# Two of four weight sums per quad formed by accumulating transfers

## The chip, the core and the metric

The kernel runs on one core of one Trainium2 chip. The metric is the time in microseconds of one execution on the device. Times of one kernel are compared as medians over runs, and where one profiled execution is read, its own time stands beside it.

## What is computed

One decoder block of a model with 1024 channels over 2048 positions, in float32:

```
proj = x @ W_in + b_in                      # 1024 -> 9216 columns
q, k, v, g_attn, u_lru, g_lru, gate_logits = split(proj)
A: rotary q, k; causal dilated window attention in 3 groups of 8 heads, merged by softmax weights,
   times silu(g_attn), @ w_attn_proj
B: width-4 causal conv of u_lru -> RG-LRU scan over positions, times silu(g_lru), @ w_lru_proj
merged = sigmoid(gA) * A + sigmoid(gB) * B
out = LayerNorm(2**0.25 * x + merged @ w_out + b_out)
```

Only the first line, `x @ W_in`, is touched by the change.

## The kernel before

The program has three stages. Stage A computes the input projection and starts what hangs on its columns (rotary parts, convolution and scan, gates). Stage B is the attention. Stage C merges and projects out. The change lies in stage A, about the first 1,550 us.

**The quad.** Stage A goes over the positions in two halves of 1024 columns and, in each half, over 36 pairs of 128-wide column tiles of `W_in`. One pair in one half is a quad: a 2 x 2 block product, with A the weights (A11 and A12 of the first tile, A21 and A22 of the second, each 128 x 512 and 256 KB) and B the positions. All but the first quad of each half are done by the Strassen-Winograd scheme, with 7 block products in place of 8. It needs four sums of weights: S1 = A21 + A22, S2 = S1 + A11, S3 = A21 + A11 and S4 = S2 + A12 (the second tile is taken with its sign turned, and `sgn` in `result` turns it back, so that all four are plain additions). `UNIT` names the weight block of each of the 7 products: A11, A12, S4, A22, S1, S2, S3. The order in a quad (`MID`) is A11, S2, S3, S1, A12, A22, S4.

Every block product is made of 12 matmuls of 128 x 512: each operand is split into a high half `h`, rounded to the matmul's format, and a low half `l`, the rest, and three of the four partial products are computed. `product` (line 577; its matmuls are line 592) issues them into one of four PSUM banks, and `evacuate` takes the bank out again on VectorE or ScalarE.

**The tick.** The whole of stage A is written out by a planner. One tick is one block product; `base[s]` is the tick at which quad s begins, and `at(t, fn)` puts an action into tick t. Each engine carries out its instructions in the order in which they are put there, so a tick fixes an order and not a time. Chains (`qk_chain`, `v_chain`, `lru` and others) take the results on; `spend` books their costs against a budget for each engine, which only decides in which tick a chain's next step is put. In the columns of u and g_lru (quads of kind "ug") the `lru` chain is started, in those of v the `v_chain`, whose four transposes `turn` stand on TensorE in the middle of a product.

**The weights of one quad.** With `t0 = base[s] - 4` in the first half and `base[s] - 3` in the second:

- `load_w` (line 237): SyncE loads A21 and A11 at t0 - 4, A22 and A12 at t0 - 3, each into one of 32 slots of 128 x 512 (`take`, `give`).
- `sums` (line 243), at t0 - 1: four additions, all on VectorE in the first half; in the second half S1 and S2 on VectorE, S3 and S4 on GpSimd (PoolE).
- `prep_w` (line 257), one for each of the seven blocks at t0 + j: ScalarE writes the high half (line 262). In the first half the low half follows, for even j on PoolE and for odd j on VectorE, and SyncE stores the low halves in `wl_scr` (line 279). In the second half SyncE loads them from there with `load_lo` (line 284).

All additions and subtractions are recorded by the helper `tt`, so they have line 232 in the profile, whatever they add; tiles tell them apart. `S<-wA,wA` is a sum of two loaded blocks (S3 and S1), `S<-S,wA` a sum with an earlier one (S2 and S4).

**Beside it.** At the start of each half the blocks of positions are split (`one_block`, line 221) and combined (`comb`: VectorE subtracts, ScalarE rounds, PoolE and VectorE write the low halves `xT`, line 221).

Of the kernel before, what the change touches and what calls it, by code (L numbers as in the profile page):

```python
# [8 lines left out]
F32 = mybir.dt.float32  # L9
F32R = mybir.dt.float32r  # L10
AF = mybir.ActivationFunctionType
ALU = mybir.AluOpType
# [3 lines left out]
P = 128  # L16
S = 2048
# [14 lines left out]
def hybrid_block_kernel(ctx: ExitStack, tc: tile.TileContext, a: dict, out: bass.AP):  # L32
    nc = tc.nc
    sp, act, dve, pool, pe = nc.sync, nc.scalar, nc.vector, nc.gpsimd, nc.tensor
# [111 lines left out]
    def take(name, dt=F32R):  # L146
        if not vacant:
            raise RuntimeError(f"no slot at {now['n']}: {[x[1].name if hasattr(x[1],'name') else x[1] for x in home.values()]} chains {len(chains)}")
        i = vacant.pop(0)
        t = sl_p.tile([P, CH], dt, tag=f"s{i}", name=name)  # L150
        home[id(t)] = (i, t)
        return t

    def give(*ts):
        for t in ts:
            vacant.append(home.pop(id(t))[0])
# [27 lines left out]
    def spend(**eng):  # L184
        for k, v in eng.items():
            left[k] = left.get(k, 0.0) - v
# [44 lines left out]
    def tt(eng, out, in0, in1, op):  # L231
        eng.tensor_tensor(out=out, in0=in0, in1=in1, op=op)  # L232


    U, LO, raw = {}, {}, {}

    def load_w(s, n):
        f = plan[s][1][int(n[1]) - 1][0]
        r = raw[s, n] = take(f"w{n}_{s}", F32)
        k = 4 * (int(n[2]) - 1)  # L240
        sp.dma_start(r.rearrange("p (k f) -> p k f", f=P), a["w_in"][f, :, k:k + 4, :])

    def sums(s):
        def add(n, x, y):
            t = raw[s, n] = take(f"{n}_{s}", F32)
            tt(pool if plan[s][0] and n in ("S3", "S4") else dve, t, raw[s, x], raw[s, y], ALU.add)
        add("S3", "A21", "A11")
        add("S1", "A21", "A22")
        give(raw.pop((s, "A21")))
        add("S2", "S1", "A11")  # L250
        add("S4", "S2", "A12")
        if plan[s][0]:
            spend(DVE=1.45, POOL=2.8)
        else:
            spend(DVE=2.9)

    def prep_w(s, j):

        n = units_of(s)[j]
        r = raw.pop((s, n))  # L260
        h = take(f"h{n}_{s}")
        act.activation(h, r, AF.Copy)  # L262
        spend(ACT=.66)
        if (s, j // 2) not in LO:
            LO[s, j // 2] = take_lo(f"l{j}_{s}")
        l = LO[s, j // 2][1][:, j % 2]
        if plan[s][2] is None or not plan[s][0]:
            eng = pool if j % 2 == 0 else dve
            tt(eng, l, r, flat(h), ALU.subtract)
            if eng is pool:  # L270
                spend(POOL=1.4)
            else:
                spend(DVE=.72)
        give(r)
        U[s, n] = (h, l)
        if plan[s][2] and not plan[s][0] and (j % 2 or j == 6):
            jj = j - j % 2
            t = LO[s, j // 2][1][:, 0:j - jj + 1]
            later(2, lambda: sp.dma_start(wl_scr[plan[s][3]][:, jj:j + 1], flat(t)))

    def load_lo(s, j):
        t = LO[s, j // 2] = take_lo(f"l{j}_{s}")
        n = 1 if j == 6 else 2
        sp.dma_start(flat(t[1][:, 0:n]), wl_scr[plan[s][3]][:, j:j + n])
# [240 lines left out]
    plan = []  # L525
# [116 lines left out]
    def at(t, fn):  # L642
        events.setdefault(t, []).append(fn)

    for s in range(1, NQ):
        t0 = base[s] - (3 if plan[s][0] else 4)
        for d, n in ((4, "A21"), (4, "A11"), (3, "A22"), (3, "A12")):
            at(t0 - d, lambda s=s, n=n: load_w(s, n))
        if plan[s][2] is None:
            for j in range(4):  # L650
                at(t0 + j, lambda s=s, j=j: prep_w(s, j))
            continue
        at(t0 - 1, lambda s=s: sums(s))
        for j in range(7):
            if plan[s][0] and j % 2 == 0:
                at(t0 + j - 1, lambda s=s, j=j: load_lo(s, j))
            at(t0 + j, lambda s=s, j=j: prep_w(s, j))
# [153 lines left out]
    sp2n = cst.tile([P, 8], F32, name="sp2n")  # L811
    left.update(PE=0.0, ACT=0.0, DVE=0.0, POOL=0.0)
    load_w(0, "A11")
    for kk in K4:
        load_raw("B11", 0, kk)
    load_w(0, "A12")
    for kk in K4:
        load_raw("B21", 0, kk)
# [49 lines left out]
    n = len(where)  # L868
# [145 lines left out]
    for m in range(NB + 4):  # L1014
        u, n = divmod(m, 16)
# [142 lines left out]
    for n in range(32):  # L1158
        c, f = divmod(n, 8)
# [23 lines left out]
    for j in range(3):  # L1183
        t = vx_p.tile([P, D], F32, name=f"vec{j}")
# [176 lines left out]
```

## Time and profile before

| | us |
|---|---|
| median of 3 runs | 2370.11 (2366.2 to 2374.58) |
| the profiled execution's own time | 2367.86 |
| span of its profile | 2366.1 |
| TensorE matmul busy | 2243.1 (95%) |
| VectorE busy | 1809.8 (76%) |
| ScalarE busy | 1086.5 (46%) |
| GpSimd busy | 953.3 (40%) |
| transfers, queue of SyncE | 64.9% of the 16 transfer engines' span |

The profile is one execution, read by the hardware profiler. PE is TensorE's matmul side and PEld its weight loads, DVE is VectorE, ACT ScalarE, POOL GpSimd, SP SyncE; a q behind an engine's name is its sequencer, which issues transfers. A wait is put down to the instruction or transfer that ended it. The time of a line is summed over the span, and an engine that stands idle costs nothing unless TensorE or the end waits for it.

### The profile page before, as it was taken

Reading aid. Unit: us, or ns where it says so; the run is one execution under the profiler, and the core shown is the slowest. Engines: PE = TensorE matmul, PEld = TensorE weight load, DVE = VectorE, ACT = ScalarE, POOL = GpSimd, SP = SyncE. Lnnn points to the kernel's source line nnn. Section 1 sums busy time; section 2 is a strip of 40 time slices with the busy share of each in tenths; the row PEclk is TensorE's granted clock in tenths of the full one; section 3 lists DMA queues with packets and bytes.
Section 4 is the critical chain, followed back from the end, with each engine's and each line's share of the span. In section 5 each row is a group of like instructions: output and inputs, shape, how many; then the busy total and the mean of one; then the engine's idle time right before and its main releaser. Section 6 shows DMA issues by size and latency. Waiting matters only on the chain. (4 is left out here: it accounts for less than half of the span.)

```text
span 2366.1 us, 34337 instructions
## 1 busy us (share of the span) xinstructions
PE 2243.1 (95%) x11008; PEld 1877.8 (79%) x11008; DVE 1809.8 (76%) x3221; ACT 1086.5 (46%) x1989; POOL 953.3 (40%) x655
## 2 busy tenths in 40 slices
PE   6999999999999999999999999999999999979998
PEld 4777777777777778888888788888999877758886
DVE  7988877888898778878879879745666558856677
ACT  4444244244344566647657657546666611121100
POOL 5443443443444623332323223378666326622220
PEclk8999999999999999999999999999999999999999
DMA  5665755766866967687687776797876579874431
GB/s 206 215 193 191 236 178 181 237 203 204 245 222 206 325 213 203 208 262 216 208 249 213 236 218 210 249 263 186 225 203 163 161 234 299 278 232 151 160 116 63
DMA packets 319237, 500.60 MB, mean 212 GB/s; under 512 B 95952, under 2 KB 136912, under 8 KB 314448
## 3 DMA queue, kind: packets, MB, share of 16 engines
q1 hardware_dynamic: 300384, 475.64, 64.9%
q10 hardware_dynamic: 18672, 22.75, 3.0%
q8 instruction: 88, 1.44, 0.3%
q14 instruction: 93, 0.76, 0.1%
HBM read 290.85 MB, written 182.26 MB: 200 GB/s over the span
## 5 line engine op out<-in xcount | busy, mean ns | idle before, releaser
L592 PE MATMUL q<-xT,hS 128*128 128x512 f32 x1680 | 525.5, 394 | 16.6 <-DVE y L232 10.3
L592 PE MATMUL q<-xT,l 128*128 128x512 f32 x1120 | 440.5, 393 | 0.5 <-DVE l L232 0.5
L592 PE MATMUL q<-xB,hA 128*128 128x512 f32 x1248 | 392.3, 396 | 22.3 <-ACT hA L262 14.8
L592 PEld LDWEIGHTS q<-xT,hS 128*128 128x128 f32 x1680 | 316.7, 190 | 88.3 <-issue 15.0
L592 PE MATMUL q<-xB,l 128*128 128x512 f32 x904 | 356.7, 395 | 3.8 <-DMA l<-wl_scr 3.6
L592 PEld LDWEIGHTS q<-xB,hA 128*128 128x128 f32 x1248 | 236.7, 191 | 72.7 <-ACT hA L262 15.7
L592 PEld LDWEIGHTS q<-xT,l 128*128 128x128 f32 x1120 | 213.1, 190 | 46.7 <-DVE l L232 1.7
L262 ACT ACTIVATE hS<-S 128x512 fp32r<-128x512 f32 x280 | 168.9, 620 | 138.6 <-DVE S L232 123.8
L232 POOL TENSOR_TENSOR l<-S,hS 128x512 fp32r<-128x512 f32 x70 | 103.9, 1484 | 277.7 <-ACT hS L262 247.5
L232 POOL TENSOR_TENSOR sw<-sw,sin 128x512 f32<-128x512 f32 x96 | 161.3, 1684 | 120.3 <-DMA sw<-y 101.9
L926 ACT ACTIVATE p<-p,osb 128x256 f32<-128x256 f32 (+1 forms) x384 | 156.2, 454 | 112.2 <-DVE osb L924 108.0
L592 PEld LDWEIGHTS q<-xB,l 128*128 128x128 f32 x904 | 172.5, 191 | 41.7 <-DMA l<-wl_scr 4.3
L924 DVE CUSTOM_DVE_ANT_0 p<-s,mask 128x256 f32<-128x256 f32 (+1 forms) x384 | 125.2, 364 | 100.2 <-PE s L920 60.5
L592 PE MATMUL q<-xB,hS 128*128 128x512 f32 x560 | 177.8, 399 | 12.5 <-DVE v L232 12.5
L592 PE MATMUL q<-xT,hA 128*128 128x512 f32 x560 | 177.6, 399 | 0.0
L959 PE MATMUL o<-V,ptb 128*128 128x65 f32 x1200 | 165.1, 276 | 10.7 <-ACT ptb L940 8.7
L959 PEld LDWEIGHTS o<-V,ptb 128*128 128x128 f32 x1200 | 151.7, 194 | 22.6 <-ACT ptb L940 19.9
L262 ACT ACTIVATE hA<-wA 128x512 fp32r<-128x512 f32 x218 | 135.4, 622 | 73.0 <-DVE y L538 13.7
L232 POOL TENSOR_TENSOR l<-wA,hA 128x512 fp32r<-128x512 f32 x74 | 116.5, 1575 | 105.2 <-ACT hA L262 92.7
L592 PEld LDWEIGHTS q<-xB,hS 128*128 128x128 f32 x560 | 105.8, 192 | 37.5 <-ACT hS L262 9.2
L592 PEld LDWEIGHTS q<-xT,hA 128*128 128x128 f32 x560 | 106.3, 192 | 21.7 <-ACT vh L455 0.3
L1213 POOL TENSOR_TENSOR me<-gA,ybr 128x512 f32<-128x512 f32 x32 | 47.2, 1489 | 183.0 <-DVE gA L1212 158.5
(187 smaller groups left out, 4917.3 us busy)
## 6 DMA issues: line engine op xcount, KB each, us to landing
wA<-in_w_in_dram SPq DMA_DIRECT2D x288, 256.0 KB, 4.2
wl_scr<-l SPq DMA_DIRECT2D x105, 512.0 KB, 4.1
l<-wl_scr SPq DMA_DIRECT2D x105, 512.0 KB, 4.9
sw<-y SPq DMA_DIRECT2D x384, 64.0 KB, 2.4
mg_scr<-y SPq DMA_DIRECT2D x59, 256.0 KB, 4.2
o_scr<-osb ACTq DMA_DIRECT2D x48, 264.0 KB, 5.8
oc<-o_scr SPq DMA_DIRECT2D x48, 264.0 KB, 4.9
v_scr<-vs SPq DMA_DIRECT2D x48, 260.0 KB, 3.7
```

Source lines behind the costliest of these rows:

```text
L232: eng.tensor_tensor(out=out, in0=in0, in1=in1, op=op)
L262: act.activation(h, r, AF.Copy)
L592: pe.matmul(bank, w[:, ks], x[:, kk, xx], start=(first and i == 0), stop=(last and i == 11))
L924: dve.tensor_tensor_reduce(out=p[:, h, lo:256], in0=s[:, h, lo:256], in1=mask[:, lo:256], scale=1.0, scalar=3e38, op0=ALU.add, op1=ALU.min ...
L926: act.activation(p[:, h, lo:256], p[:, h, lo:256], AF.Exp, scale=-1.0, bias=mm)
L959: pe.matmul(o[:, n % 2, h * 65:h * 65 + 65], ptb[:, 2 * h + x, :], V[:, kb, vo + h * 65:vo + h * 65 + 65], start=(x == lo // P), stop=(x = ...
L1213: pool.tensor_tensor(out=ME[c][:, f], in0=ga, in1=yb, op=ALU.add)
```

## The change

S1 and S3 are no longer added by an engine. A21 is loaded twice, into the slot of S1 and into that of S3, at t0 - 6. At t0 - 4 PoolE issues two transfers that add what they bring to what is in the slot: A22 onto S1, A11 onto S3. A11, A22 and A12 are loaded as before. S2 and S4 are added on VectorE in both halves. So per quad SyncE issues 5 loads in place of 4, PoolE issues 2 transfers, VectorE does two additions (four before in the first half, two in the second) and PoolE none (two before in the second half). The planner's booking for the sums falls to 1.8 on VectorE. There are 70 such quads.

```
     def load_w(s, n):
+        r = raw[s, n] = take(f"w{n}_{s}", F32)
+        sp.dma_start(r.rearrange("p (k f) -> p k f", f=P), w_part(s, "A21" if n[0] == "S" else n))
+
+    def w_part(s, n):
+
         f = plan[s][1][int(n[1]) - 1][0]
-        r = raw[s, n] = take(f"w{n}_{s}", F32)
         k = 4 * (int(n[2]) - 1)
-        sp.dma_start(r.rearrange("p (k f) -> p k f", f=P), a["w_in"][f, :, k:k + 4, :])
+        return a["w_in"][f, :, k:k + 4, :]
+
+    def added(s, n, x):
+
+        t = raw[s, n].rearrange("p (k f) -> p k f", f=P)
+        pool.dma_start(t, w_part(s, x), accum_op=ALU.add)
 
     def sums(s):
         def add(n, x, y):
             t = raw[s, n] = take(f"{n}_{s}", F32)
-            tt(pool if plan[s][0] and n in ("S3", "S4") else dve, t, raw[s, x], raw[s, y], ALU.add)
-        add("S3", "A21", "A11")
-        add("S1", "A21", "A22")
-        give(raw.pop((s, "A21")))
+            tt(dve, t, raw[s, x], raw[s, y], ALU.add)
         add("S2", "S1", "A11")
         add("S4", "S2", "A12")
-        if plan[s][0]:
-            spend(DVE=1.45, POOL=2.8)
-        else:
-            spend(DVE=2.9)
+        spend(DVE=1.8)
...
     for s in range(1, NQ):
         t0 = base[s] - (3 if plan[s][0] else 4)
-        for d, n in ((4, "A21"), (4, "A11"), (3, "A22"), (3, "A12")):
-            at(t0 - d, lambda s=s, n=n: load_w(s, n))
         if plan[s][2] is None:
+            for d, n in ((4, "A21"), (4, "A11"), (3, "A22"), (3, "A12")):
+                at(t0 - d, lambda s=s, n=n: load_w(s, n))
             for j in range(4):
                 at(t0 + j, lambda s=s, j=j: prep_w(s, j))
             continue
+        for d, n in ((6, "S1"), (6, "S3"), (4, "A11"), (3, "A22"), (3, "A12")):
+            at(t0 - d, lambda s=s, n=n: load_w(s, n))
+        at(t0 - 4, lambda s=s: added(s, "S1", "A22"))
+        at(t0 - 4, lambda s=s: added(s, "S3", "A11"))
         at(t0 - 1, lambda s=s: sums(s))
```

## The prediction

> **What bounds the kernel now.** I read the page first, then busy times by stage, then what TensorE waited for in each half of stage A, then the groups of additions, then the timeline at one stall.
>
> ```profile
> span 2366.1 us, 34337 instructions
> PE 2243.1 (95%) x11008; PEld 1877.8 (79%) x11008; DVE 1809.8 (76%) x3221; ACT 1086.5 (46%) x1989; POOL 953.3 (40%) x655
> ...
> core 0: us, PE busy (x) PEld busy (x) DVE busy (x) ACT busy (x) POOL busy (x), PEclk, DMA share, GB/s
> 0.00:39.60 39.60, 24.77 (x96) 19.62 (x96) 27.48 (x37) 18.40 (x30) 23.01 (x23) 0.96 0.78 280
> 39.60:78.30 38.70, 29.16 (x85) 20.75 (x86) 32.26 (x55) 20.86 (x36) 17.41 (x12) 0.73 0.32 97
> 78.30:802.60 724.30, 686.89 (x3002) 560.39 (x3001) 610.50 (x726) 302.94 (x519) 306.25 (x198) 0.98 0.67 217
> 802.60:854.40 51.80, 43.05 (x182) 34.85 (x181) 41.19 (x46) 28.90 (x50) 25.91 (x17) 0.93 0.64 226
> 854.40:1553.00 698.60, 694.91 (x3097) 573.96 (x3096) 568.78 (x739) 432.41 (x705) 221.41 (x148) 1.00 0.76 227
> 1553.00:2366.10 813.10, 764.30 (x4553) 668.22 (x4552) 529.57 (x1620) 282.97 (x652) 359.28 (x259) 0.98 0.65 195
> ```
>
> The rows are: the plain first quad, the first Winograd quad, the 34 quads after it, the change of half with its first quads, 34 quads of the second half, and stages B and C, which the change does not touch. TensorE is the bound. In the second half it has 3.7 us idle in 698.60: nothing is to be had there. In the first half the same 34 quads take 724.30 us though they hold fewer matmuls:
>
> ```profile
> L466 PE MATMUL g<-vh,gw 128*128 128x512 f32 x16 | 6.2, 390 | 0.0
> ...
> L466 PE MATMUL g<-vh,gw 128*128 128x512 f32 x48 | 18.7, 389 | 0.0
> ```
>
> The first row is the first half, the second row the second. Lines 464 and 465 have the same counts, so the second half does 3 x 32 = 96 matmuls more. At its pace (694.91 / 3097 = 0.224 us) these are 21.5 us. The first half thus wastes 724.3 - 698.6 + 21.5 = 47 us. This is the most that relief of another engine can give. What it waits for (first three rows: first half; last row: all of the second):
>
> ```profile
> PE vtp L352 <- DVE y L538: 18.5, 6, 4.4
> PE q L592 <- DVE y L232: 10.3, 9, 2.2
> PE q L592 <- DVE v L232: 8.6, 8, 1.3
> ...
> PE q L592 <- DMA l<-wl_scr: 3.6, 1, 3.6
> ```
>
> 37.4 us are VectorE being late, either with the y that the four transposes of `v_chain` turn, or with a bank. One such place, first VectorE, then TensorE:
>
> ```profile
> 130.04 2.88 DVE L232 TENSOR_TENSOR S<-wA,wA 128x512 f32<-128x512 f32 x2
> 132.95 1.42 DVE L232 TENSOR_TENSOR S<-S,wA 128x512 f32<-128x512 f32 x2
> 134.28 0.68 DVE L232 TENSOR_TENSOR v<-u,q 128x512 f32<-128x512 f32 x1
> ...
> 135.48 0.75 DVE L538 SCALAR_TENSOR_TENSOR y<-q,bn,v 128x512 f32<-128x512 f32 x1
> ...
> 136.28 1.11 PE L352 MATMUL vtp<-ident,y 128*128 128x128 f32 x4 [4.41 <-DVE y L538]
> ```
>
> The four sums stand directly ahead of the y for which TensorE has stopped.
>
> **Part 1: two additions leave VectorE, first half.**
>
> ```profile
> L232 DVE TENSOR_TENSOR S<-wA,wA 128x512 f32<-128x512 f32 x66 | 81.9, 1277 | 0.5 <-DMA wA<-in_w_in_dram 0.4
> L232 DVE TENSOR_TENSOR l<-wA,hA 128x512 fp32r<-128x512 f32 x35 | 32.9, 939 | 56.1 <-ACT hA L262 49.0 <-DMA wA<-in_w_in_dram 7.1
> ```
>
> S1 and S3 are the row of 66: 2 x 1.277 = 2.55 us per quad, 81.9 us in the stage. At the six transposes this is 2.88 us against waits of 3.1 on average and 4.4 at most: I count 17 of 18.5 us. The 17 bank waits are at most 2.2 us, less than 2.55, and go altogether: 18.9. Together 36 us; the shorter stops also cost less of the clock (up to the 47), and new waits, below, take a little. I take **-35**, bounds 0 and -47. The bound of 0 is there because the second row shows VectorE itself waiting 49 us for ScalarE's high halves: that is late next.
>
> **Part 2: the second half.** VectorE keeps two sums per quad, so nothing leaves it. PoolE loses S3 and S4, which nobody on the path waited for: 0 gain, since TensorE has nothing left to gain.
>
> **Part 3: PoolE issues 140 transfers.** The trace has no transfer from PoolE. From below, SyncE's issue; from above, PoolE's longest group; between them its own shortest addition:
>
> ```profile
> L241 SPq DMA_DIRECT2D wA<-in_w_in_dram x16: 328/328/743, 0.7 to 79.3; - x16
> ...
> L770 POOL TENSOR_TENSOR C<-C,B 64x1024 fp32r<-64x1024 f32 x48 | 113.6, 2366 | 3.5
> ...
> L232 POOL TENSOR_TENSOR S<-S,wA 128x512 f32<-128x512 f32 x33 | 42.8, 1297 | 134.3 <-DVE S L232 92.2 <-PE q L592 12.3 <-ACT hS L262 12.0
> ```
>
> 0.33 to 2.37 us each; I take 1.3, as PoolE must make the transfer itself. 2 x 1.3 per quad is some 90 us in 724, and PoolE is busy for 306 there: it fits. Behind the two transfers PoolE has the low halves `l` of the quad before. Those are written four ticks (11 us at 12 x 0.224 per tick) before TensorE wants them, and no row of either half has TensorE waiting for PoolE. That slack hides the issues and a short wait for the loads, which SyncE puts two ticks (5.4 us) earlier. Without that cover each quad would pay 2.6 us.
>
> **Part 4: when the sum is there.** The transfer is issued at t0 - 4, the addition S2 that reads S1 stands at t0 - 1: three ticks, 8.1 us.
>
> ```profile
> wA<-in_w_in_dram SPq DMA_DIRECT2D x288, 256.0 KB, 4.2
> ...
> l<-wl_scr SPq DMA_DIRECT2D x105, 512.0 KB, 4.9
> ...
> A<-ql_scr SPq DMA_DIRECT2D x24, 512.0 KB, 11.0
> ```
>
> From below a load of the same size, 4.2; from above the slowest of twice the size, 11.0, if the slot must be read as well as written. I take 6, nearest the 512 KB load at 4.9 with some queue. 1.3 + 6 = 7.3 is inside 8.1, and VectorE is behind its tick whenever TensorE waits for it: **0**. The Trainium skill ("DMA: Bandwidth & Descriptors", Anatomy of one DMA — SWDGE (gpsimd) path) gives about 2.0 us plus bytes / 436 GB/s for a transfer that GpSimd issues, an estimate of 2.6 us for 256 KB; our SyncE load of that size took 4.2, and by 2.6 the sum would stay the same. No run here shows a PoolE transfer.
>
> **Part 5: the start.** PoolE takes its instructions in order, and the first two transfers stand ahead of the low half of A21 of quad 0:
>
> ```profile
> 13.87 1.74 POOL L232 TENSOR_TENSOR l<-wA,hA 128x512 fp32r<-128x512 f32 x1
> 17.69 6.39 POOL L221 TENSOR_TENSOR xB<-xB,xB 128x512 fp32r<-128x512 f32 x4 [2.08 <-ACT xB L220]
> 25.38 2.97 POOL L221 TENSOR_TENSOR xT<-xcB,xT 128x512 fp32r<-128x512 f32 x2 [1.29 <-ACT xT L220]
> ...
> 15.69 1.00 SPq L241 DMA_DIRECT2D wA<-in_w_in_dram  x2
> ...
> DMA to landing us min/median/max: 2.8/5.3/5.6
> ...
> 27.14 1.76 DVE L232 TENSOR_TENSOR xcB<-xcB,xcB 128x512 f32<-128x512 f32 x1 [1.18 <-POOL xT L221]
> 30.81 1.29 DVE L232 TENSOR_TENSOR S<-wA,wA 128x512 f32<-128x512 f32 x2
> ...
> 70.33 1.29 DVE L232 TENSOR_TENSOR S<-wA,wA 128x512 f32<-128x512 f32 x2
> ```
>
> S1 and S3 take the place of the two loads at 15.69, so the second lands at 16.2 + 5.3 = 21.5. Then PoolE issues twice: about 24 us, when the `l` at 13.87 starts, 10 us later. The blocks at 17.69 end at 24 + 1.7 + 6.4 = 32 in place of 24, so `xT` starts at 32 in place of 25.4: 6.6 us later, and VectorE at 27.14 waits for it. The first Winograd quad hangs on that chain (9.5 us idle on TensorE). VectorE is spared two additions (1.29 us) at 30.81 and at 70.33: 6.6 - 2.6 = **+4**, bounds 0 and +10. At the change of half the same order holds, with the loads asked for earlier: half of it, **+2**, bounds 0 and +5.
>
> **Part 6: the transfers' load.** Per quad one more 256 KB load and two adding transfers. In the second half the share is 0.76 at 227 GB/s, so full is about 299 GB/s; 34 x 3 x 0.262 MB over 698.6 us is +38 GB/s, a share of 0.89, and if the slots' reading counts too, +64 and 0.97. TensorE has waited there once for `l<-wl_scr`, 3.6 us. I take two more such waits, **+8**; from below 0, from above one in each of the eight "ug" groups, +29. A rule of the Trainium skill speaks against the change here ("Collectives: The Full Stack", The bandwidth ceiling: the fold count): an adding transfer needs two source reads and so runs at half the rate of a copy. By it the share is the 0.97; no transfer in this trace adds.
>
> **Sum.** -35 + 0 + 4 + 2 + 8 = -21 against this execution's own 2367.9 (span 2366.1; the median of the three runs is 2370.1, 0.1% above): **2347 us**.
>
> **Rivals.**
>
> - *The transfers fill the second half.* The spare share there is 0.24 x 299 x 698.6 = 50 MB, 5.6 loads of 0.262 MB per quad. One goes to the extra load, so an adding transfer that costs more than 2.3 loads makes this half wait for transfers. At 3 loads each quad overruns by 1.4 loads, 1.2 us, 42 us in all: 2367.9 - 35 + 6 + 42 = 2381. For it: the share of 0.76 already. Against it: two is the natural price of one more read.
> - *The sum lands late.* If a transfer takes the 11 us of the slowest row, S2 stands on VectorE for 11 + 1.3 - 8.1 = 4 us less VectorE's own lag, and behind it all evacuations. The 2.55 us per quad are given back and the rest of the sum stays: 2367.9 + 14 = 2382. It decides from a landing of about 8 to 9 us. Against it: no 256 KB row has such a median.
> - *Another wait follows at once.* VectorE's waits for ScalarE's high halves (49 us) grow by what the sums free, and a third of the gain is left: 2367.9 - 12 + 14 = 2370, no change.
>
> That the change does not do what it says is out: the instruction order has 70 additions fewer on VectorE and 70 more entries each on PoolE and SyncE.
>
> **How the numbers follow.** Forecast 0.52 (own range 2321 to 2360: from the full 47 without costs to two thirds of the 35 with costs of 14), transfers full 0.21, late sums 0.14, another wait 0.13. 0.3% (7 us) is about what a measurement here can tell from no change. Faster 0.52, same 0.13, slower 0.35. Range 2322 to 2386: all but the tails of the two slow cases and of the full gain.
>
> **What would show it.** Right: the `vtp` waits fall below 5 us, the first half's 34 quads take about 690 us, the second half's 700 to 710, PoolE's transfers last 1 to 1.5 us, and the first Winograd quad ends about 4 us later. Wrong: VectorE waiting at `S` for a transfer, a share near 1 in the second half, TensorE waiting for PoolE's `l`, or a PoolE transfer of several us.

## The result, and the profile after

| | before | after |
|---|---|---|
| median of 5 runs, us | 2369.89 | 2392.35 |
| ratio, 95% interval | | 1.0084 (1.0061 to 1.0106) |
| profiled execution's own time, us | 2367.86 | 2389.12 |
| its span, us | 2366.1 | 2387.3 |

The changed kernel is slower by 0.84%; 2347 had been forecast, with a range that ended at 2386. One of its five executions took 5578.71 us; it is left out of the ratio (the median of the other four is 2390.7), and its cause stays open.

The span and the busy times come first, then the windows of the five stages, cut as in the prediction (start and first Winograd quad together, 34 quads of the first half, change of half, 34 quads of the second half, stages B and C):

```profile
span 2387.3 us, 34689 instructions
PE 2252.9 (94%) x11008; PEld 1877.8 (79%) x11008; DVE 1739.7 (73%) x3151; ACT 1087.7 (46%) x1989; POOL 961.9 (40%) x725
...
0.00:78.40 78.40, 52.11 (x180) 38.28 (x181) 54.93 (x87) 37.74 (x64) 40.64 (x38) 0.87 0.66 216
78.40:789.30 710.90, 684.37 (x3001) 555.38 (x3000) 572.89 (x661) 303.54 (x521) 363.33 (x265) 0.99 0.87 257
789.30:840.00 50.70, 43.62 (x182) 35.30 (x181) 38.11 (x47) 28.45 (x49) 22.60 (x17) 0.93 0.75 249
840.00:1569.00 729.00, 702.87 (x3097) 574.56 (x3096) 544.13 (x739) 434.29 (x706) 173.71 (x147) 0.99 0.89 254
1569.00:2387.30 818.30, 769.97 (x4553) 674.29 (x4552) 529.63 (x1620) 283.69 (x652) 361.58 (x260) 0.97 0.65 194
```

VectorE does 70 us less work in all, 38 of them in the first half, and TensorE, the bound, still needs longer. The difference of the spans, 21.2 us, comes out of these rows and those of before:

| stage | before | after | difference |
|---|---|---|---|
| start and first Winograd quad | 78.3 | 78.4 | +0.1 |
| first half | 724.3 | 710.9 | -13.4 |
| change of half | 51.8 | 50.7 | -1.1 |
| second half | 698.6 | 729.0 | +30.4 |
| B and C | 813.1 | 818.3 | +5.2 |

So the first half gained a third of what was expected of it, and the second, where 8 us had been feared, lost 30. The +5.2 in B and C can't be put down to the change: over the thirteen kernels of this case, none of which touches these stages, they take 809.9 to 818.3.

What TensorE waited for in the first half (first three rows) and in the second (last three):

```profile
PE g L468 <- DVE vl L232: 11.5, 8, 2.0
PE q L595 <- DVE y L232: 9.0, 11, 1.4
PE vtp L355 <- DVE y L541: 1.7, 3, 0.8
...
PE q L595 <- DMA l<-wl_scr: 16.9, 10, 2.6
PE vtp L355 <- DVE y L541: 8.2, 3, 3.7
PEld q L595 <- DMA l<-wl_scr: 22.8, 15, 3.0
```

The columns are the wait's total, its count and the longest, in us. The stops at the transposes fell from 18.5 to 1.7 us, as forecast, but a new wait of 11.5 us for VectorE's `vl`, the low half that the gate matmuls `g` read, stands in their place. In the second half, TensorE had waited 3.6 us for the low halves read back from `wl_scr`; now it is 16.9, and its weight loads (PEld) wait for them too. The 30.4 us are 22 us more idle time (4 before, 26 now) and 8 us more in matmuls that run longer (694.9 to 702.9).

The queues and landings (first row: SyncE's queue, second: PoolE's; then count, size and median us from issue to landing), and VectorE's and PoolE's waits in the second half:

```profile
q1 hardware_dynamic: 310464, 494.00, 66.2%
q0 software_dynamic: 20160, 36.71, 9.4%
...
wA<-in_w_in_dram SPq DMA_DIRECT2D x218, 256.0 KB, 5.4
l<-wl_scr SPq DMA_DIRECT2D x105, 512.0 KB, 5.9
wS<-in_w_in_dram POOLq DMA_DIRECT2D x140, 256.0 KB, 6.6
sw<-y SPq DMA_DIRECT2D x384, 64.0 KB, 3.7
...
DVE S L232 <- DMA wA<-in_w_in_dram: 33.3, 18, 4.7
POOL wS L250 <- DMA wS<-in_w_in_dram: 84.6, 11, 16.8
```

The transfers that were there before land later: a weight block after 5.4 us (4.2 before), the low halves after 5.9 (4.9). In the second half VectorE now stands 33 us for a weight block, and PoolE 85 us for the blocks onto which its transfers are to add. The 33 us are two waits, of S2 (first row) and S4 (second):

```profile
L232 DVE TENSOR_TENSOR S<-wS,wA 128x512 f32<-128x512 f32 x33 | 25.3, 767 | 19.0 <-DMA wA<-in_w_in_dram 9.9 <-DMA wS<-in_w_in_dram 6.6 <-issue 2.5
L232 DVE TENSOR_TENSOR S<-S,wA 128x512 f32<-128x512 f32 x33 | 22.9, 692 | 25.9 <-DMA wA<-in_w_in_dram 23.4 <-DMA mg_scr<-y 1.8
```

### The profile page after: what moved, and what is told of

Same layout as the page of the kernel before. It is cut to its first block, busy times and chain, and to the rows that moved or that the text cites. A ratio compares the mean times of both kernels' runs of the same rounds, so it can differ in the third digit from the quotient of the medians.

```text
span 2387.3 us, 34689 instructions
## 1 busy us (share of the span) xinstructions
PE 2252.9 (94%) x11008; PEld 1877.8 (79%) x11008; DVE 1739.7 (73%) x3151; ACT 1087.7 (46%) x1989; POOL 961.9 (40%) x725
## 3 DMA queue, kind: packets, MB, share of 16 engines
q0 software_dynamic: 20160, 36.71, 9.4%
## 4 chain that ended last, share of the span: by engine, by line
PE 43%; DMA 21%; DVE 15%; issue 8%; SPq 5%; ACT 5%; POOL 2%; DVEq 0%; ACTq 0%; POOLq 0%
PE q L595 22%; PE o L966 4%; DMA wA<-in_w_in_dram 4%; DMA sw<-y 3%; SPq L307 3%; PE s L927 3%; DVE y L232 2%; DMA wS<-in_w_in_dram 2%; PE z L1248 2%; PE z L1246 2%; PE z L1247 2%; PE pt L942 2%; DVE rp L232 2%; DMA A<-qh_scr 1%; PE yb L1155 1%
## 5 line engine op out<-in xcount | busy, mean ns | idle before, releaser
L595 PEld LDWEIGHTS q<-xT,hS 128*128 128x128 f32 x1680 | 315.5, 189 | 87.8 <-issue 14.3
L595 PE MATMUL q<-xB,l 128*128 128x512 f32 x904 | 356.7, 395 | 26.0 <-DMA l<-wl_scr 16.9
L250 POOL DMA_DIRECT2D wS<-in_w_in_dram x140 | 123.4, 978 | 337.4 <-DMA wS<-in_w_in_dram 105.0
L927 PE MATMUL s<-B,A 128*128 128x256 f32 (+1 forms) x384 | 118.0, 328 | 8.9 <-DMA A<-qh_scr 7.0
L232 DVE TENSOR_TENSOR y<-y,cos 128x512 f32<-128x512 f32 x96 | 101.3, 1056 | 33.3 <-DMA sw<-y 31.6
```

The source lines that it names most:

```text
L250: pool.dma_start(t, w_part(s, x), accum_op=ALU.add)
L595: pe.matmul(bank, w[:, ks], x[:, kk, xx], start=(first and i == 0), stop=(last and i == 11))
L927: pe.matmul(s[:, h, (0 if g == 2 and n else lo):256], q, k, start=(i == 0), stop=(i == 1))
```

## The experiments

Four things are mixed in the change: the relief of VectorE in the first half; 786 KB more traffic per quad; that two of the transfers add; and the order of work on two engines, since in the second half S4 goes from PoolE to VectorE and PoolE stands for SyncE's loads. The theories: either the bare traffic fills the second half (T1 in the expectations), or it is the adding, or the moved waits. The kernels below take these apart. All differences in the text are between the same stretches of 34 quads, in one profiled execution of each kernel.

A fifth thing comes with the change, and no kernel below changes it alone: the booking. With 1.8 booked for the sums on VectorE in place of 2.9 (first half), the planner puts steps of the chains into other ticks. The traces show it in the order of the instructions. In the first half the eight groups of gate matmuls `g` stand one product earlier on TensorE in the changed kernel, in `e_first`, `e_plain` and `f_s4pool`, but in their old place in `e_second`, `e_traffic`, `f_wait` and `b_pool`. At the stall that the prediction shows, a group `g` now stands ahead of the transposes, and TensorE stops there instead:

```profile
135.22 0.39 PE L467 MATMUL g<-vh,gw 128*128 128x512 f32 x1
137.47 0.50 PE L468 MATMUL g<-vl,gw 128*128 128x512 f32 x1 [1.86 <-DVE vl L232]
...
138.92 0.66 PE L355 MATMUL vtp<-ident,y 128*128 128x128 f32 x4
```

This holds at four of the six transposes that had stopped TensorE: stops of 14.1 us in all became stops of 7.7 us at `g`. The order of all instructions other than the sums is the same in the changed kernel, `e_plain` and `f_s4pool`, and, in the first half, in the kernel before and `e_traffic`. Differences inside these two groups have nothing to do with the booking; differences across them, and to `b_pool`, can have.

**One half at a time.** `e_first` and `e_second` have the change in the first and in the second half alone.

```
+    def by_dma(s):
+        return not plan[s][0]        # e_first;  e_second: return plan[s][0]
...
+        if by_dma(s):
             at(t0 - 4, lambda s=s: added(s, "S1", "A22"))
             at(t0 - 4, lambda s=s: added(s, "S3", "A11"))
```

(`sums` and the loads go by `by_dma` in the same way.)

> The change in the first half alone; the second half has its four loads and four engine additions back. Theory T1 (the added transfers lengthen every other landing, and the second half pays for it in transfers of low halves and swaps): the second half's 34 quads return to about 700 us from 729, the first half keeps its 711, total 2367.9 - 13 = 2355 (the ratio 0.994). Rival T2 (the order on PoolE and SyncE of the whole of stage A, or something outside stage A): the total stays above 2370. If stages B and C also fall back from 818 to 813, their 5 us belonged to the change in the second half.

> The change in the second half alone. If the two halves add up, the first half is back at 724, the second at 727 to 729, total about 2367.9 + 30 + 5 = 2400 (ratio 1.013). T1 and its rivals agree on this; it tells whether the loss hangs on anything done in the first half: then the total would stay near 2370.

`e_first`: 2357.97 us, 0.9938 (0.9919 to 0.9957). `e_second`: 2399.95, 1.0116 (1.0094 to 1.0137). The windows of the two halves, of `e_first` and then of `e_second`:

```profile
79.30:790.40 711.10, 682.36 (x3001) 554.35 (x3001) 571.68 (x661) 303.24 (x521) 365.95 (x265) 1.00 0.87 257
842.20:1542.40 700.20, 694.43 (x3097) 573.38 (x3096) 569.55 (x739) 432.75 (x705) 220.97 (x147) 1.00 0.76 226
...
76.60:804.50 727.90, 689.48 (x3002) 562.27 (x3001) 611.70 (x726) 303.32 (x519) 305.40 (x198) 0.98 0.67 216
855.20:1584.70 729.50, 704.38 (x3097) 574.58 (x3096) 546.18 (x739) 433.81 (x705) 172.81 (x147) 0.99 0.89 253
```

Both came out as expected. Each half behaves as in the full change (711.1 and 729.5, against 710.9 and 729.0), and the other half nearly as before (700.2 and 727.9, against 698.6 and 724.3). The change is a small gain and a larger loss, each got without the other. Stages B and C take 811.6 us in `e_first` and 814.0 in `e_second`.

**The traffic without the change.** `e_traffic` is the kernel before, with three loads per quad more that nobody reads: one by SyncE, two by PoolE, none of which adds.

```
+        at(t0 - 6, lambda s=s: spare(s, "A21", sp))
+        at(t0 - 4, lambda s=s: spare(s, "A22", pool))
+        at(t0 - 4, lambda s=s: spare(s, "A11", pool))
         at(t0 - 1, lambda s=s: sums(s))
```

> The kernel before, with all four sums on the engines, and three unused 256 KB loads per quad beside it: one from SyncE at t0 - 6, two plain ones from PoolE at t0 - 4, into slots that nobody reads. T1 (traffic alone lengthens the landings): the second half's 34 quads go from 699 to 715 to 730 us and the first half's from 724 to 735 to 745 (waits for swaps, as the changed kernel shows 27 us of them, with nothing gained), total 2395 to 2420. Rival T2 (PoolE's wait for the loads ahead of its sums, and the sums' own lateness): total within 8 us of 2368.

2384.78 us, 1.0056 (1.0038 to 1.0075). Its two halves, and TensorE's waits in the first (three rows) and the second (one row):

```profile
79.40:815.20 735.80, 689.87 (x3002) 561.79 (x3001) 617.49 (x726) 303.46 (x518) 339.32 (x263) 0.98 0.78 248
866.90:1565.70 698.80, 694.40 (x3098) 571.70 (x3097) 563.76 (x739) 434.15 (x706) 252.54 (x211) 1.00 0.86 264
...
PE vtp L359 <- DVE y L545: 19.9, 6, 3.7
PE q L599 <- DVE y L232: 13.7, 12, 2.0
PE q L599 <- DVE v L232: 12.3, 9, 1.6
...
PE q L599 <- DMA l<-wl_scr: 2.8, 3, 1.2
```

The second half takes the traffic for nothing (698.8 at a share of 0.86 and 264 GB/s, more bytes per second than in the changed kernel): the bare load as the cause of the +30 falls. The first half, where the prediction had priced no load, pays 11.5 us (7.9 beside `e_second`, whose first half is that of the kernel before), and it pays them in longer waits for VectorE, which is itself busy for 617.5 us there in place of 610.5. The run doesn't part the bytes from the 33 us that PoolE spends more (339.3 against 306.3). The first half is as T1 had it, the second is not, and the total fits neither theory.

**The adding taken away.** `e_plain` is the changed kernel whose PoolE transfers overwrite in place of adding; it leaves the sums S1 and S3 out, so its time stands for the same order of instructions and the same bytes without the adding.

```
-        pool.dma_start(t, w_part(s, x), accum_op=ALU.add)
+        pool.dma_start(t, w_part(s, x))
```

> As changed, but PoolE's transfers overwrite the slot and do not add (S1 becomes A22, S3 becomes A11, so the sums are left out); order, waits and bytes brought are the same. If the adding itself (a second read of the slot, half rate) is the load: the share in the second half falls from 0.89 towards 0.83, PoolE's landing from 6.6 to about 5 us, and the total by 10 us or more to below 2380. If it is the three more transfers as such or their waits (T1 without a price for adding): the same within 5 us, 2385 to 2392.

2355.01 us, 0.992 (0.9894 to 0.9945). Halves, PoolE's queue, the landing, TensorE's wait for the low halves and VectorE's for a weight block (both second half):

```profile
78.90:776.80 697.90, 680.94 (x3002) 554.91 (x3001) 569.18 (x660) 301.26 (x520) 339.99 (x265) 0.99 0.82 262
827.40:1543.40 716.00, 701.32 (x3098) 576.10 (x3097) 539.19 (x739) 432.51 (x702) 152.98 (x147) 0.99 0.84 257
...
q0 software_dynamic: 11200, 36.71, 5.2%
...
wS<-in_w_in_dram POOLq DMA_DIRECT2D x140, 256.0 KB, 4.9
...
PE q L595 <- DMA l<-wl_scr: 6.3, 8, 1.6
DVE S L232 <- DMA wA<-in_w_in_dram: 38.9, 21, 5.3
```

Adding costs 13.0 us in the first half (697.9 to 710.9) and 13.0 in the second (716.0 to 729.0). The same 36.71 MB keep the transfer engines busy for 5.2% of the span, 9.4% when they add; the waits for `wl_scr` grow from 6.3 to 16.9 us. This is what was expected if the adding is the load. But 17 of the 30 us of the second half are left with nothing added, and VectorE's wait for a weight block is left whole.

**S4 back on PoolE.** Most of that wait, 23.4 of 33.3 us in the changed kernel, is of S4, which needs A12, the quad's last load; the rest is of S2, for A11. `f_s4pool` is the changed kernel with the second half's S4 on PoolE, where it was before.

```
-            tt(dve, t, raw[s, x], raw[s, y], ALU.add)
+            tt(pool if plan[s][0] and n == "S4" else dve, t, raw[s, x], raw[s, y], ALU.add)
```

> As changed, but S4 of the second half stays on PoolE as in the kernel before. Three unused loads cost the second half nothing (698.8 us) and transfers that overwrite cost it 17 us, so what is left of its 30 us beside the adding (13) is a wait. Theory T3: it is S4 = S2 + A12, which the change moves to VectorE, where it waits for A12, the last load (33.3 us of waits at S in the changed kernel): the second half falls from 729 to about 712, VectorE's waits at S for wA fall below 10, total about 2372. Rival T4: PoolE, which stands at its transfers until the loads land, and so comes late to the rotary product of the swaps: the second half stays at 725 to 732, total 2385 to 2395.

2378.52 us, 1.0043 (1.0028 to 1.0058). Second half, and in it VectorE's wait for a weight block and TensorE's two waits:

```profile
839.70:1556.80 717.10, 700.77 (x3098) 572.81 (x3097) 530.80 (x706) 433.08 (x703) 221.20 (x181) 1.00 0.90 258
...
DVE S L232 <- DMA wA<-in_w_in_dram: 14.3, 6, 3.8
...
PE q L595 <- DMA l<-wl_scr: 15.8, 12, 2.8
PE vtp L355 <- DVE y L541: 0.2, 1, 0.2
```

VectorE's wait falls from 33.3 to 14.3 us and the half by 11.9, while the waits for `wl_scr` stay: two causes side by side. That the 11.9 go by way of VectorE is seen at the transposes, where TensorE's wait falls from 8.2 to 0.2. This is theory T3 in the main, though short of its 712, 10 and 2372: the 14.3 us left are S2's. But the run takes the addition's own 22.9 us off VectorE as well as its wait, so it doesn't part the two. That the kernel before has two additions there as well, and TensorE only 3.7 us idle, speaks for the wait.

**PoolE standing for a load.** `f_wait` is `e_traffic` with one difference: PoolE's first unused transfer goes into the slot of SyncE's unused load, so PoolE must wait for it, as in the change.

```
+        if n == "A22":
+            t = held.pop(s)               # the slot that SyncE filled with A21
+        else:
+            t = take(f"x{n}_{s}", F32)
```

> The kernel before with its four engine additions and three unused 256 KB transfers per quad, but the first of PoolE's two plain transfers now goes into the slot that SyncE's unused load has just filled, so PoolE stands still until that load has landed, as in the changed kernel; no sum reads the slot. T4 (PoolE's waiting in order): the second half's 34 quads go from 699 to 710 to 716 us, total 2395 to 2405. T3 (S4 on VectorE): it stays at 698 to 702, total within 5 us of the 2385 of the run without the wait.

2389.76 us, 1.0093 (1.007 to 1.0116). The second half, and PoolE's wait:

```profile
868.50:1574.20 705.70, 696.03 (x3098) 570.97 (x3097) 563.39 (x739) 433.50 (x706) 250.92 (x212) 1.00 0.85 262
...
POOL xA L252 <- DMA xA<-in_w_in_dram: 77.6, 23, 8.1
```

6.9 us beside `e_traffic` (698.8), with 77.6 us of standing, about what PoolE has in the changed kernel (84.6). The first half is the same (735.5 against 735.8). This lies between what T4 (710 to 716) and T3 (698 to 702) expected. Here PoolE still has its two sums behind the transfers, which it doesn't have in the changed kernel, so the 7 us are carried over and not measured there. So the second half's loss is adding 13, S4 on VectorE 12 and PoolE's standing about 7, together 32 where 30.4 were lost; the three were each measured against another neighbour, so they need not add up exactly.

**A fourth cause that was not borne out.** In the first half of the changed kernel VectorE waits for the rotary swap, which goes through a transfer (first row; second: for ScalarE's high halves):

```profile
DVE y L232 <- DMA sw<-y: 27.4, 14, 4.3
DVE l L232 <- ACT hA L265: 35.2, 20, 3.2
```

So I took the swap, landing after 3.7 us in place of 2.4, for what held the first half at 711. `e_first_lag` gives it a tick more, `e_lag` does so in the full change, and `b_lag` in the kernel before, as the control.

```
-        yield Ask(lag=2, DVE=.75, POOL=1.4)
+        yield Ask(lag=3, DVE=.75, POOL=1.4)
```

> The change in the first half alone, and the rotary step of every chain put one tick later after its swap transfers (lag 3 in place of 2). In the first half of the changed kernel VectorE waits 27.4 us for swaps. If that is what holds back the first half's gain (711 us where relief without traffic should give 686): those waits fall below 8, the first half comes to 690 to 700 us, total 2342 to 2350. If the traffic costs by other landings: 708 to 713 and 2355 to 2360.

> The control of the run with lag 3: the kernel before, nothing of the change, the rotary step one tick later. If the later step gains by the waits for swaps that the transfers' load brought (27 us in the changed kernel's first half, 1 us in the kernel before): total within 5 us of 2367. If the step gains by itself, by where it puts VectorE's work: the first half falls by 10 us or more, total below 2355, and the gain of e_first_lag over e_first may not be put down to the swaps.

> The change in both halves with the rotary step one tick later. If what it does in the first half (711 to 681.5 us) is the same here, the first half comes to 680 to 685; the second half, which is held back by S4 on VectorE, the adding and PoolE's standing, and not by swaps on VectorE, stays at 720 to 730. Total 2352 to 2365. If the second half falls to 710 or less, the swaps were part of its loss too.

`e_first_lag`: 2328.31, 0.9835 (0.9808 to 0.9862). `b_lag`: 2329.87, 0.9843 (0.9815 to 0.9871). `e_lag`: 2361.22, 0.997 (0.9953 to 0.9987). First halves of the three in this order, then the second half of `e_lag`:

```profile
79.20:760.70 681.50, 671.12 (x3002) 554.13 (x3001) 546.55 (x661) 305.74 (x521) 351.12 (x265) 1.00 0.90 268
...
77.70:770.30 692.60, 675.12 (x3002) 554.53 (x3002) 600.87 (x726) 302.61 (x519) 305.78 (x198) 1.00 0.69 226
...
78.70:769.00 690.30, 677.96 (x3001) 558.22 (x3000) 548.63 (x661) 306.04 (x521) 349.04 (x265) 0.99 0.89 265
819.60:1547.40 727.80, 702.52 (x3097) 571.35 (x3096) 549.33 (x739) 433.37 (x705) 172.84 (x146) 1.00 0.89 254
```

The control gains 32 us in its first half with nothing of the change in it, and hardly any wait for swaps there: the gain of `e_first_lag`, larger than expected, can't be put down to the swaps. What the later step does is put VectorE's work into other ticks, in every kernel. So where the planner puts the work is worth as much in this half as the sums are. With the later step the change's first half is worth 11 us by `e_first_lag` (692.6 to 681.5), 2 by `e_lag` (690.3, where 680 to 685 were expected), and nothing in the whole time (2328 and 2330). These two have the same order of instructions in that half and still differ by 8.8 us, so a difference of that size between two single executions is not sure. The loss in the second half is untouched (727.8), as expected.

**Two additions moved without a transfer.** `b_pool` is the kernel before with S3 and S4 on PoolE in both halves, as it has them in the second. As in the change, two additions per quad leave VectorE in the first half, though one is another.

```
-            tt(pool if plan[s][0] and n in ("S3", "S4") else dve, t, raw[s, x], raw[s, y], ALU.add)
+            tt(pool if n in ("S3", "S4") else dve, t, raw[s, x], raw[s, y], ALU.add)
...
-        if plan[s][0]:
-            spend(DVE=1.45, POOL=2.8)
-        else:
-            spend(DVE=2.9)
+        spend(DVE=1.45, POOL=2.8)
```

> The kernel before with S3 and S4 on PoolE in the first half too, as it has them in the second: the same two additions leave VectorE there, without any transfer. PoolE then has 306 + 34 x (1.5 + 1.3) = 400 us of 724 in that stage. If VectorE's relief is worth 38 us when nothing is paid for it, and PoolE can take it: the first half falls to 690 us, total 2333 to 2340. If PoolE's additions hold VectorE's two-operand instructions up or its low halves come late: 705 to 730, total 2350 to 2375.

> S3 and S4 on PoolE in both halves and the rotary step one tick later; no adding transfer. b_pool has only 7 us of TensorE idle left in the first half (681.0 against 673.7 busy), so at most that much more: first half 676 to 682, second half 694 to 700, total 2310 to 2321. If the step was only a cure for the transfers' load: equal to b_pool within 3 us.

2321.33 us, 0.9802 (0.9778 to 0.9826): the fastest kernel of this case. Its first half, and TensorE's longest wait there:

```profile
75.20:756.20 681.00, 673.71 (x3001) 555.09 (x3000) 584.37 (x660) 303.59 (x520) 405.19 (x265) 1.00 0.72 231
...
PE vtp L349 <- DVE y L535: 5.8, 5, 2.6
```

43 of the 47 us that the prediction gave as the most that relief can bring are got, more than expected, with two additions leaving VectorE for PoolE and not one byte more. TensorE's order is that of the kernel before; VectorE's is not, as the booking changes here too, so the 43 us are not the additions' alone for sure. The later step on top, `b_pool_lag` (the two edits above together), misses its expectation: 2325.89, 0.9826 (0.9801 to 0.9852), with a first half of 694.7. The two gains do not add; why the half gets worse stays open.

## Why the prediction was wrong

Two steps failed, each for about as much: the load that Part 6 left out of the first half, and the second half, which Part 2 put at 0 and Part 6 at +8.

- **Part 6, the load: a step that failed.** It priced the load for the second half alone and nothing for the first, without a reason. The first paid 11.5 us for the traffic and 13.0 for the adding, so 24.5 us went back. In the second half the traffic alone costs 0 and the adding 13, against the +8 taken; that part of the mechanism, TensorE waiting for `wl_scr`, was right. That its 0.89, for the share with the slots' reading left out, was measured is luck: with plain transfers the share is 0.84 to 0.86, and the adding brings it to 0.89. What the reading costs is seen in the queue, 1.8 times the engine time.
- **Part 2, "nothing leaves it ... 0 gain": the other step that failed.** It counted additions and found two before and two after. But S1, S2 became S2, S4, and S4 reads A12, the last of the loads, issued two ticks ahead of the sums. On PoolE no row had TensorE waiting for it; on VectorE it has the evacuations behind it: 12 us with S4's own time in them.
- **Part 1, the relief: right in size, in part by luck.** -35 was forecast. At equal traffic, from `e_traffic` to `e_plain`, the first half goes from 735.8 to 697.9: -37.9. But these two differ in the booking too, and how much of the 37.9 is the relief stays open. Nor was VectorE relieved as Part 1 counts it: it put the two sums at 81.9 us, and VectorE's busy time fell by 37.6, because much of what stayed took longer (S2 and S4 together 72.1 us in place of 57.5; why stays open). The `vtp` waits fell to 1.7, below the 5 named, partly because `g` now stands ahead of them and TensorE waits there.
- **Part 3, the issues: price right, cover wrong.** The group's row gives 978 ns each, with 337.4 us of idle time before them, 105.0 of it for the loads that they add to:

```profile
L250 POOL DMA_DIRECT2D wS<-in_w_in_dram x140 | 123.4, 978 | 337.4 <-DMA wS<-in_w_in_dram 105.0
```

  1.3 had been taken. The issue of a plain transfer is hidden, since `e_traffic` issues as many and its second half loses nothing. "A short wait for the loads" is not short: up to 16.8 us, 85 in the second half, worth about 7 there if `f_wait` stands for it.
- **Part 4, when the sum is there: right in its figures.** 6 us were taken and 6.6 measured; VectorE waits for `wS` three times in the whole span, 8.1 us. The rival of the late sum did not come about. VectorE waits at `S`, which was named as a sign of error, but for plain loads, the last one above all.
- **Part 5, the start: a miss without weight.** +4 and +2 came out as +0.1 and -1.1.
- **The rivals.** The one that filled the second half gave 2381 and the late sum 2382, near the measured time by other ways. The first set 42 us for an adding transfer that costs as much as three loads. It costs 1.8 plain ones, under the 2.3 that were to decide, and the half lost 30 by smaller causes. The third, that VectorE's waits for ScalarE's high halves grow, did not come about: they fell from 49.0 to 35.2 us.

Together: -35 and +14 forecast, -38 (with what the booking did) and +59 found: 24.5 in the first half, 30.4 in the second, and the rest in stages that scatter by as much.

## What to carry to other kernels

When an addition changes its engine, follow what it reads as well as what it costs: VectorE had two sums before and two after, but one of the new two waits for the last load, and taking it away again gave 12 us back. Price added traffic in every stage, above all in those where the bound engine already waits, and not only where the share is highest. Before transfers are made to do arithmetic, try the engine that has time left: moving two of the four additions to GpSimd brought 2%, where the transfers lost 0.8%. And where a planner places work by booked costs, change the booking by itself too: a later step alone brought 1.6% here, and part of what looks like relief may be placement.

## What the runs showed of the hardware

An adding transfer is dear at the transfer engines and at its issuer. The queue rows above give 9.4 / 5.2 = 1.8 times the engine time for the same 36.71 MB, in 144 packets for each transfer against 80. The Trainium skill says of the reducing step of a collective that its add reads two sources and so runs at half a copy's rate ("Collectives: The Full Stack", The bandwidth ceiling: the fold count); what is measured here comes close to that. The issue on GpSimd is longer too, in the changed kernel and then in `e_plain` (shortest, median and longest in ns):

```profile
L250 POOL DMA_DIRECT2D wS<-in_w_in_dram x140: 850/878/1207, 20.8 to 1534.7; - x140
...
L250 POOL DMA_DIRECT2D wS<-in_w_in_dram x140: 536/538/709, 21.5 to 1508.4; - x140
```

Landing took 6.6 against 4.9 us. The estimate of 2.6 us that was worked out from the Trainium skill ("DMA: Bandwidth & Descriptors", Anatomy of one DMA — SWDGE (gpsimd) path) is exceeded even by the plain transfers, in a kernel where other transfers run beside them.

And a share of 0.86 at 264 GB/s cost the second half nothing, while 0.78 cost the first 11.5 us. In these runs the share of the transfer engines did not tell by itself whether more traffic hurts. That the slack of those who wait for it decides is my reading: TensorE was idle for 3.7 us in the second half before and for 37.4 in the first. No run varies that slack alone.
